# One transformer layer on one core: the gate projection `vg` computed with seven block products instead of eight, with its factors, its row statistics and the spatial weights prepared at other places

## The chip, the cores and the metric

The kernel runs on one core of one Trainium2 chip. TensorE (PE) does the matmuls and the transposes, VectorE (DVE), ScalarE (ACT) and GpSimd (POOL) the element-wise work, and SyncE (SP), POOL and in one place ACT issue the transfers, which 16 DMA engines carry out. The metric is the device time of one execution in microseconds (us), lower is better; several runs are given by their median.

## The reference

One layer of a streaming encoder, `x` of 512 rows (tokens) by 2048, all in fp32:

```python
h = rms_norm(x, g_mix)
proj = h @ w_in                      # 2048 x 9216
q, k, v_sb, u, v_sg, gate_a, gate_b = split(proj, [1024, 1024, 1024, 1024, 1024, 2048, 2048])
y_a = stick_breaking_attention(rms_norm(q), rms_norm(k), v_sb) @ w_oa      # 8 heads
v_sg = gelu(v_sg)
s = gelu(u) * (w_spatial(masked) @ layer_norm(v_sg) + b_spatial)           # 128-token chunks, 8 groups
y_b = s @ w_ob
merged = sigmoid(gate_a) * y_a + sigmoid(gate_b) * y_b
x = x + merged @ w_out
x = x + square(relu(rms_norm(x, g_ff) @ w_ff1)) @ w_ff2
```

The change is about `v_sg` (1024 of the 9216 columns; the kernel calls it `vg`): `rms_norm(x) @ w_in[:, vg]`, its gelu, and the mean and variance of each row that the layer norm needs.

## The kernel before

**Arithmetic.** Every fp32 operand is split in a high and a low part, and a product is the sum of three matmuls: high by high, high by low, low by high (`mm3`, L70 to L74). A weight "piece" is 512 KB, 128 partitions by 1024: it is loaded into a raw tile (pool `raws`, six tiles), ACT casts it to its high part, and DVE takes the difference as its low part (`weight`, L92 to L103; `split_to`, L111 to L117). The parts lie in a pool of three pairs (`w_piece`). Activations lie in `slots`, 64 tiles of 128x512, and in `long`, 12 more. PSUM has five banks for sums (`acc`) and three for side work (`aux`).

**Order of the work.** The program is written in the order of the stages, and each engine runs its instructions strictly in a fixed order, which a scheduler draws up at compile time from a simulated timeline; the transfers of a queue are issued in that order too. Side tasks are put in a queue, `behind`; `step()` (L81) takes one task after each weight piece, or after each of the seven products of a Strassen form. A task's place is thus given by its step.

**Stages.** At the start `x` is loaded in four quarters of 512 columns. `hT_of(k)` (L439) makes the transposed, scaled activations of k-tile k when they are first asked for: four PE transposes into one bank, then two ACT and two DVE instructions of 128x256, whose results are the high and the low part. `by_token` (L122) computes 512 columns of the projection for all four token blocks, eight pieces and 192 matmuls of 128x512 a pass. The first two passes give `v` (8 to 104 us of the profile), and the next two give `vg` (104.4 to 192.75 us), each with 192 matmuls. `evac_v` (L720) then applies the gelu (L722), takes the statistics (`bn_stats`, L723) and puts the result in DRAM (`held_v`, L724).

From 192.76 us on comes a long "run" of gates and attention heads (`strassen_pair`, L277, with `strassen_columns`, L215): for two column tiles and the two halves of the k rows, seven block products in the order y11, m7, m6, y21, m5, m4, y22. The activations of the products are h's own four blocks (y11, y12, y21, y22) and four combinations of them (m7, m6, m4, m5: the "factors", `factor`, L245), kept for eight k pairs. `gate_factors(k)` makes those of one pair: four additions that join high and low part again (`whole`, L514), four sums or differences (L251) and the halves again (ACT and DVE). Before, the eight calls stand at steps 3, 5, ... 17 of the second `v` pass, so most of them fall in the `vg` stage.

Because `long` takes its room from the start, the activations of k-tiles 6, 7 and 8 lie in raw tiles (`hT_both`), and `moved` (L670) copies them to slots by DMA later. The spatial weights are loaded, transposed, masked and split (`load_spatial`, L629; `spatial`, L640) in the second `v` pass. `open_gates` (L715) starts the run's first weight loads in the last step of `vg`.

**The form for rows.** Near the end of the middle part, `w_out` (about 975 to 1125 us) is computed with `strassen_tokens` (L303): four quarters, each with seven products over 1024 weight rows and 1024 columns; a product is 24 matmuls of 128x512. Two of the seven weight operands are sums that DVE makes from raw pieces (L186, L190), and two more are made by transfers that add into a raw tile (POOL queue, L188, L201). Each product's bank is added to one or two of the four results, by ACT where the result is new (L945) and by DVE else (L947).

Of the kernel before, what the change touches and what calls it, by code (L numbers as in the profile page):

```python
# [31 lines left out]
RAWH = 3  # L32
# [3 lines left out]
def tile_hybrid_layer(ctx: ExitStack, tc: tile.TileContext, x, g_mix, w_in, g_q, g_k, ln_g, ln_b,  # L36
# [12 lines left out]
    first = ExitStack()  # L49
    long = first.enter_context(tc.tile_pool(name="long", bufs=LONG))  # L50
# [25 lines left out]
    state = {"load": None, "raw": raws}  # L76
# [362 lines left out]
    def hT_of(k):  # L439

        if k == len(hT):
            t = aux("xT")
            for tb in range(NTB):
                nc.tensor.transpose(out=t[:, tb * P:(tb + 1) * P], in_=xq[tb, k], identity=ident)
# [46 lines left out]
    for k in range(CK):  # L491
# [137 lines left out]
    def load_spatial():  # L629
        for half in range(2):  # L630
            t = slot("ws")
            nc.sync.dma_start(out=t.rearrange("p (g j) -> p g j", g=4),
# [3 lines left out]
            nc.sync.dma_start(out=t, in_=b_sp.rearrange("o g i -> o (g i)")[:, half * W:(half + 1) * W]  # L636
# [3 lines left out]
    def spatial(half):  # L640
        t = aux("wsT")
# [10 lines left out]
        rows = aux("rows")  # L652
        for i in range(2):
# [3 lines left out]
            nc.sync.dma_start(out=held_s[half * 2 + i], in_=f32(pair))  # L657
# [8 lines left out]
        nc.sync.dma_start(out=held_s[4 + half], in_=bs[half])  # L666
# [3 lines left out]
    def moved(k):  # L670
        for half, part in enumerate(hT[k]):
            name = "y" + "12"[k % 2] + "12"[half]
            if LONG // 2 <= k < LONG // 2 + RAWH and name != "y12":
                t = slot("hT", F32R)
                nc.sync.dma_start(out=f32(t), in_=f32(part))
                part = t
            hy[name, k // 2] = part
# [40 lines left out]

    for half in range(2):
        def evac_v(tb, o):  # L720
            t = room.pop() if room else slot("vg")
            state["gelu"] = nc.scalar.activation(out=t, in_=o, func=AF.Gelu, scale=rstd[:, tb:tb + 1])  # L722
            nc.vector.bn_stats(out=stv[:, tb, half * 6:half * 6 + 6], in_=t)  # L723
            nc.gpsimd.dma_start(out=held_v[half, tb], in_=t)  # L724

        if half:
            behind.extend([lambda: None] * (KT // CK - 1 - len(behind)))
            behind.append(open_gates)
        by_token(win, VS + half * W, hT_at, KT, evac_v, "vg", turn=half * LONG // 2)
# [21 lines left out]
    behind.append(moments)  # L751
# [131 lines left out]
    for j in range(D // W):  # L883
        def evac_b(c, o):
# [41 lines left out]
    CHUNK = 4  # L926
    ready = ({"y21": [(0, 0)], "m4": [(0, 1)], "m5": [(1, 1)], "y22": [(1, 0)]}, done[1])

    class Merged:


        def __init__(self, f):
            self.f = f

# [245 lines left out]
```

## Time and profile before

| | us |
|---|---|
| three runs | 2397.48, 2398.22, 2398.96 (median 2398.22) |
| the profiled execution's own time | 2400.23 |
| its span, first to last instruction | 2398.5 |
| opening and `v`, two passes | to 104.4 |
| `vg`, two passes | 104.4 to 192.75 |
| start of the run | 192.76 |

All views are of one profiled execution, with times from the start of its span. A row of a group gives the line, the engine, the operation, what is written and read, the count, then the busy time and the mean duration of one in ns, then the idle time of the engine just before and what ended it. A timeline row gives start, duration, engine, line and operation. A window row gives its length, the busy time of PE, its weight loads, DVE, ACT and POOL with the number of instructions, the granted clock of PE (1.00 is full), the busy share of the DMA engines and GB/s.

### The profile page before, as it was taken

How to read it: one execution, taken by the hardware profiler on the slowest of the kernel's cores; microseconds unless marked ns; L12 is line 12 of the kernel's file. 1: busy time of each engine (PE TensorE's matmuls, PEld its weight loads, DVE VectorE, ACT ScalarE, POOL GpSimd, SP SyncE). 2: the span in 40 equal slices, each digit the busy share in tenths (PEclk: the TensorE clock that was granted, in tenths of full speed). 3: DMA queues.
4: the chain of work that ended last, by engine and by line, in shares of the span. 5: the costliest groups of instructions: out<-in, count | busy, mean ns of one | idle time of the engine just before them, and what ended most of it. 6: DMA issues, size and time to landing. Idle time of an engine off the chain costs nothing.

```text
span 2398.5 us, 34712 instructions
## 1 busy us (share of the span) xinstructions
PE 2382.6 (99%) x12436; PEld 2046.4 (85%) x12436; DVE 1948.1 (81%) x2670; ACT 1340.2 (56%) x2094; POOL 516.6 (22%) x631
## 2 busy tenths in 40 slices
PE   9999999999999999999999999999999999999999
PEld 8888888888888888888988888888888788888887
DVE  5576887778788567778689888898888898998987
ACT  5335676666666323458667777777765343333333
POOL 0101222222222433231000000000024334321210
PEclk9999999999999999999999999999999999999999
DMA  5557888888888945497388888889887999877763
GB/s 185 194 162 161 168 175 188 170 185 171 183 166 191 350 152 180 117 223 198 93 237 229 233 230 226 224 225 230 230 292 264 308 269 318 249 222 213 229 185 96
DMA packets 513037, 498.84 MB, mean 208 GB/s; under 512 B 20896, under 2 KB 398816, under 8 KB 512864
## 3 DMA queue, kind: packets, MB, share of 16 engines
q1 hardware_dynamic: 380880, 332.48, 43.6%
q0 software_dynamic: 131696, 163.61, 33.1%
q8 instruction: 98, 1.61, 0.3%
q10 hardware_dynamic: 288, 0.52, 0.1%
q14 instruction: 75, 0.61, 0.1%
HBM read 405.83 MB, written 89.65 MB: 207 GB/s over the span
## 4 chain that ended last, share of the span: by engine, by line
PE 96%; DMA 1%; DVE 1%; ACT 1%; issue 0%; POOL 0%; SPq 0%; DVEq 0%; ACTq 0%; POOLq 0%
PE q L223 18%; PE fork L223 13%; PE q L73 10%; PE q L74 10%; PE q L72 10%; PE q L226 9%; PE fork L226 7%; PE v L72 1%; PE v L74 1%; PE v L73 1%; PE vg L72 1%; PE vg L74 1%; PE yb L72 1%; PE yb L74 1%; PE yb L73 1%; PE vg L73 1%
## 5 line engine op out<-in xcount | busy, mean ns | idle before, releaser
L113 ACT CAST w_hi<-w_raw 128x1024 fp32r<-128x1024 f32 (+1 forms) x688 | 722.9, 1051 | 774.3 <-PE q L73 373.0
L114 DVE TENSOR_TENSOR w_lo<-w_raw,w_hi 128x1024 fp32r<-128x1024 f32 (+1 forms) x688 | 839.0, 1221 | 213.7 <-ACT w_hi L113 198.4
L73 PE MATMUL q<-w_lo,ys 128*128 128x512 f32 x1120 | 437.4, 391 | 3.7 <-DVE w_lo L114 3.6
L74 PE MATMUL q<-w_hi,ys 128*128 128x512 f32 x1120 | 436.2, 390 | 0.0
L223 PE MATMUL q<-ys,w_hi 128*128 128x512 f32 x1632 | 411.1, 394 | 3.6 <-ACT fork L231 3.6
L72 PE MATMUL q<-w_hi,ys 128*128 128x512 f32 x1120 | 393.1, 390 | 0.2 <-DVE total L1122 0.2
L223 PEld LDWEIGHTS q<-ys,w_hi 128*128 128x128 f32 x1632 | 293.9, 189 | 57.3 <-ACT fork L231 4.4
L73 PEld LDWEIGHTS q<-w_lo,ys 128*128 128x128 f32 x1120 | 210.4, 188 | 49.6 <-DVE w_lo L114 6.3
L72 PEld LDWEIGHTS q<-w_hi,ys 128*128 128x128 f32 x1120 | 210.3, 188 | 43.8 <-issue 0.6
L74 PEld LDWEIGHTS q<-w_hi,ys 128*128 128x128 f32 x1120 | 210.4, 188 | 43.3
L223 PE MATMUL fork<-ys,w_hi 128*128 128x512 f32 x944 | 236.2, 392 | 0.0
L226 PEld LDWEIGHTS q<-ys,w_lo 128*128 128x128 f32 x1632 | 221.3, 191 | 14.1
L188 POOL DMA_DIRECT2D w_raw<-in_w_ff_dram x57 | 79.3, 1392 | 709.7 <-ACT act L1011 160.2
L226 PE MATMUL q<-ys,w_lo 128*128 128x256 f32 x1632 | 228.0, 283 | 0.0
L223 PEld LDWEIGHTS fork<-ys,w_hi 128*128 128x128 f32 x944 | 171.5, 189 | 31.5
L1073 POOL DMA_DIRECT2D ys<-store x224 | 126.7, 578 | 185.9 <-PE q L74 121.8
L186 DVE TENSOR_TENSOR w_raw<-w_raw 128x1024 f32<-128x1024 f32 x98 | 119.7, 1222 | 39.2 <-DMA w_raw<-in_w_in_dram 10.6
L99 ACT CAST w_hi<-w_raw 128x1024 fp32r<-128x1024 f32 x71 | 74.6, 1051 | 120.4 <-issue 36.4
L101 DVE TENSOR_TENSOR w_lo<-w_raw,w_hi 128x1024 fp32r<-128x1024 f32 x71 | 87.7, 1237 | 61.7 <-ACT w_hi L99 59.9
L226 PEld LDWEIGHTS fork<-ys,w_lo 128*128 128x128 f32 x944 | 128.8, 191 | 9.2
L1122 DVE SCALAR_TENSOR_TENSOR total<-q,plus,total 128x512 f32<-128x512 f32 x180 | 132.1, 746 | 4.2 <-PE q L74 4.1
L226 PE MATMUL fork<-ys,w_lo 128*128 128x256 f32 x944 | 131.7, 283 | 0.0
(264 smaller groups left out, 3660.0 us busy)
## 6 DMA issues: line engine op xcount, KB each, us to landing
w_raw<-in_w_ff_dram SPq DMA_DIRECT2D x256, 512.0 KB, 5.8
w_raw<-in_w_in_dram SPq DMA_DIRECT2D x143, 512.0 KB, 5.3
ys<-store POOLq DMA_DIRECT2D x224, 256.0 KB, 6.7
w_raw<-in_w_ff_dram POOLq DMA_DIRECT2D x57, 512.0 KB, 7.0
w_raw<-in_w_in_dram POOLq DMA_DIRECT2D x56, 512.0 KB, 6.5
store<-ys_hi SPq DMA_DIRECT2D x90, 256.0 KB, 5.2
store<-ys_lo SPq DMA_DIRECT2D x90, 256.0 KB, 5.1
w_raw<-in_w_out_dram SPq DMA_DIRECT2D x32, 512.0 KB, 5.2
```

The lines of the kernel that those rows point to most:

```text
L72: nc.tensor.matmul(o, lhsT=lh[0], rhs=rh[0], start=start, stop=False, **kw)
L73: nc.tensor.matmul(o, lhsT=lh[0], rhs=rh[1], start=False, stop=False, **kw)
L74: nc.tensor.matmul(o, lhsT=lh[1], rhs=rh[0], start=False, stop=stop, **kw)
L101: nc.vector.tensor_tensor(out=lo, in0=raw, in1=f32(hi), op=ALU.subtract)
L113: nc.scalar.copy(out=hi, in_=src)
L114: state["lo"] = nc.vector.tensor_tensor(out=lo, in0=src, in1=f32(hi), op=ALU.subtract)
L186: nc.vector.tensor_tensor(out=self.a, in0=self.w11, in1=self.w21, op=ALU.add)
L188: state["sum"] = nc.gpsimd.dma_start(out=self.w21, in_=self.blocks[1, 1], accum_op=ALU.add)
L223: nc.tensor.matmul(o, lhsT=hi[:, k, :], rhs=rhs[name][k], start=name in ("y11", "m7") and k == 0, stop=False, skip_group_check=True)
L226: nc.tensor.matmul(o[:, :HS], lhsT=lo[:, k, :], rhs=rhs[name][k][:, :HS], start=False, stop=k == KH - 1, skip_group_check=True)
L1073: nc.gpsimd.dma_start(out=f32(t), in_=store[f][HELD.index(name), p])
L1122: nc.vector.scalar_tensor_tensor(out=a, in0=o, scalar=part, in1=a, op0=ALU.mult, op1=ALU.add)
```

## The change

1. `vg` is computed by `strassen_tokens`, in two passes over 1024 rows of the weights each, with all 1024 columns: seven products of 24 matmuls a pass. A pass takes the factors of four k pairs. The eight results (`sum`) gather in slots, in pass one and two; the gelu follows when a result is complete, and `bn_stats` is put off to the first eight steps of the run (`moment`).
2. The factors have to be there for it, so `gate_factors` stands at steps 5, 7, 9, 10, 12, 14, 16, 18, counted from the start of `v` (a `v` pass has eight steps). The slots don't suffice for all: of the first four pairs the tiles m6, y21 and m5 (twelve) are written to DRAM (`held_f`) and fetched back into `long` behind `vg`.
3. `long` opens only then; in the opening its room is a pool `more0` of six raw tiles, for the weights of `vg`. All of h lies in slots from the start; `moved` and `hT_both` are gone.
4. `load_spatial` comes after `moments` in the run, `spatial(0)` and `spatial(1)` six and ten steps later, on the banks of `acc`, with their transfers on POOL's queue.
5. The tables of `strassen_tokens` (`takes`, `done`, `ready`) and the class `Chunk` stand further up and serve `vg` and `w_out`.

```diff
+    zero = ExitStack()
+    more = zero.enter_context(tc.tile_pool(name="more0", bufs=6))
...
-            if LONG // 2 <= k < LONG // 2 + RAWH:
-                both = raws.tile([P, 2, W], F32R, name="hT_both", tag="w_raw")
-                parts = [both[:, 0, :], both[:, 1, :]]
-            else:
-                parts = [slot("hT", F32R, long if k < LONG // 2 else slots) for _ in range(2)]
+            parts = [slot("hT", F32R) for _ in range(2)]
...
-        t = aux("wsT")
+        t = acc("wsT")
...
+    PARKED = ("m6", "y21", "m5")
+    held_f = dram.tile([len(PARKED), 4, P, W], F32, name="held_f")
     def gate_factors(k):
+        for i in range(2):
+            for half, part in enumerate(hT[2 * k + i]):
+                hy["y" + "12"[i] + "12"[half], k] = part
         act = [whole(2 * k + i) for i in range(2)]
         for name in ("m7", "m6", "m4", "m5"):
             factor(hy, act, k, name, -1.0 if name in ("m7", "m4") else None)
+        if k < 4:
+            for i, name in enumerate(PARKED):
+                nc.gpsimd.dma_start(out=held_f[i, k], in_=f32(hy[name, k]))
...
-            steps[0].append(load_spatial)
-            steps[2].append(lambda: spatial(0))
-            steps[4].append(lambda: spatial(1))
-            for k in range(KT // 2):
-                steps[3 + 2 * k].append(lambda k=k: gate_factors(k))
...
+    for k, n in enumerate((5, 7, 9, 10, 12, 14, 16, 18)):
+        opening[n].append(lambda k=k: gate_factors(k))
+    opening[29].append(open_gates)
+    at_steps(opening)
...
-        by_token(win, VS + half * W, hT_at, KT, evac_v, "vg", turn=half * LONG // 2)
...
+    def gather(sums, key, o, op, flip=False):
+        if flip:
+            op = ALU.subtract if op == ALU.add else ALU.add
+        if key not in sums:
+            sums[key] = slot("sum")
+            nc.scalar.activation(out=sums[key], in_=o, func=AF.Copy, scale=1.0 if op == ALU.add else -1.0)
+        else:
+            nc.vector.tensor_tensor(out=sums[key], in0=sums[key], in1=o, op=op)
+    vg, moment = {}, []
+    for f in range(2):
+        def evac_v(name, t, o):
+            for half, c, op in takes[name]:
+                gather(vg, (2 * half + t, c), o, op, name in ("m7", "m4"))
+            for half, c in ready[0].get(name, []) if f else []:
+                tb = 2 * half + t
+                g = vg[tb, c]
+                state["gelu"] = nc.scalar.activation(out=g, in_=g, func=AF.Gelu, scale=rstd[:, tb:tb + 1])
+                nc.gpsimd.dma_start(out=held_v[c, tb], in_=g)
+                moment.append(lambda g=g, tb=tb, c=c: nc.vector.bn_stats(out=stv[:, tb, c * 6:c * 6 + 6], in_=g))
+        strassen_tokens(win, f * CHUNK * 2 * P, VS, Chunk(hy, f), evac_v, lambda name: None, twice=True)
+    zero.close()
+    first = ExitStack()
+    long = first.enter_context(tc.tile_pool(name="long", bufs=LONG))
+    for i, name in enumerate(PARKED):
+        for k in range(4):
+            hy[name, k] = fetched(held_f[i, k], "ys", F32R, long)
...
-    behind.append(moments)
+    behind.extend(moment)
+    behind.extend([moments, load_spatial] + [lambda: None] * 5 + [lambda: spatial(0)] + [lambda: None] * 3
+                  + [lambda: spatial(1)])
```

The scheduler's order on three queues shows what moves. On SP's queue in the opening, before, the last three quarters of `x` (`xq`) stand between single pieces of the weights of `v` (`w_raw`); `xk` is the first quarter, `gm` and `gains` are small vectors:

```order
L411 DMA xk<-in_x_dram 128x4x128 x3
L96 DMA w_raw<-in_w_in_dram 128x2x512
L421 DMA xq<-in_x_dram 128x512 x4
L96 DMA w_raw<-in_w_in_dram 128x2x512
L421 DMA xq<-in_x_dram 128x512 x4
L96 DMA w_raw<-in_w_in_dram 128x2x512
L421 DMA xq<-in_x_dram 128x512 x4
L396 DMA gains<-in_g_ff_dram 16x128
```

On the same queue after the change (lines of the changed kernel; L95 loads a piece of `v`, L180 one of `vg`'s first pass into `more0`); three pieces of `v` and the gains stand ahead of these rows:

```order
L95 DMA w_raw<-in_w_in_dram 128x2x512
L420 DMA xq<-in_x_dram 128x512 x4
L95 DMA w_raw<-in_w_in_dram 128x2x512 x3
L180 DMA w_raw<-in_w_in_dram 128x2x512
L95 DMA w_raw<-in_w_in_dram 128x2x512
L180 DMA w_raw<-in_w_in_dram 128x2x512 x3
L95 DMA w_raw<-in_w_in_dram 128x2x512 x2
L420 DMA xq<-in_x_dram 128x512 x8
```

The second quarter of `x` moves behind four pieces, and the third, with the fourth right after it, behind fourteen, of which four are of `vg`.

On ACT in the fifth to seventh pieces of `v`, before, activations (`hT`), squares of `x` (`sq`) and casts of weights (`w_hi`) follow one another:

```order
L436 ACTIVATE sq,ss<-xq 128x512 x4
L116 ACTIVATE hT<-xT,gT 128x256
L99 CAST w_hi<-w_raw 128x1024
L116 ACTIVATE hT<-xT,gT 128x256 x3
L436 ACTIVATE sq,ss<-xq 128x512 x4
```

At the same place after the change, where `whole` and `ys` are the first factors' tiles:

```order
L435 ACTIVATE sq,ss<-xq 128x512 x4
L115 ACTIVATE ys<-whole 128x256
L112 CAST ys<-whole 128x256
L98 CAST w_hi<-w_raw 128x1024
L115 ACTIVATE ys<-whole 128x256
L112 CAST ys<-whole 128x256
L115 ACTIVATE hT<-xT,gT 128x256 x4
```

The activations of k-tiles 12 and 13, the last row, now stand behind four instructions of the factors and behind a cast of a weight piece.

On POOL's queue from the end of `vg` into the run, before, the eight results go to DRAM and the run's adding transfers (L188, L201) follow:

```order
L724 DMA held_v<-vg 128x512 x4
L188 DMA w_raw<-in_w_in_dram 128x8x128
L724 DMA held_v<-vg 128x512 x4
L201 DMA w_raw<-in_w_in_dram 128x8x128
L737 TENSOR_TENSOR rv<-ve,mhalf 128x4
```

The same place after the change, with the adding transfers of `vg`'s second pass (128x2x512) and the twelve fetches (L509):

```order
L743 DMA held_v<-sum 128x512 x2
L200 DMA w_raw<-in_w_in_dram 128x2x512 x2
L187 DMA w_raw<-in_w_in_dram 128x8x128
L743 DMA held_v<-sum 128x512 x2
L509 DMA ys<-held_f 128x512 x12
L743 DMA held_v<-sum 128x512 x3
L200 DMA w_raw<-in_w_in_dram 128x8x128
L743 DMA held_v<-sum 128x512
L760 TENSOR_TENSOR rv<-ve,mhalf 128x4
```

The fetches stand among the results of the second pass, ahead of the last four, and ahead of the run's second adding transfer.

More of the change, by code (lines that the diff above doesn't have):

```diff
@@ L74, in mm3 @@
         nc.tensor.matmul(o, lhsT=lh[1], rhs=rh[0], start=False, stop=stop, **kw)
-    state = {"load": None, "raw": raws}
+    state = {"load": None, "raw": raws, "more": more}
     behind = collections.deque()
@@ L635, in load_spatial @@
             t = slot("bs")
-            nc.sync.dma_start(out=t, in_=b_sp.rearrange("o g i -> o (g i)")[:, half * W:(half + 1) * W]
+            nc.gpsimd.dma_start(out=t, in_=b_sp.rearrange("o g i -> o (g i)")[:, half * W:(half + 1) * W]
                               .to_broadcast([P, W]))
@@ L656, in spatial @@
             split_to(p3[:, :, 0, :], p3[:, :, 1, :], m3[:, 2 * i:2 * i + 2, :])
-            nc.sync.dma_start(out=held_s[half * 2 + i], in_=f32(pair))
+            nc.gpsimd.dma_start(out=held_s[half * 2 + i], in_=f32(pair))
             r2 = rows[:, i * 2 * P:(i + 1) * 2 * P].rearrange("p (g i) -> p g i", g=2)
@@ L665, in spatial @@
                                            in1=bs[half][:, c], op0=ALU.mult, op1=ALU.add)
-        nc.sync.dma_start(out=held_s[4 + half], in_=bs[half])
+        nc.gpsimd.dma_start(out=held_s[4 + half], in_=bs[half])
     hy = {}
[L670 to L677, printed above, removed]
+    PARKED = ("m6", "y21", "m5")
+    held_f = dram.tile([len(PARKED), 4, P, W], F32, name="held_f")
     def gate_factors(k):
+        for i in range(2):
+            for half, part in enumerate(hT[2 * k + i]):
+                hy["y" + "12"[i] + "12"[half], k] = part
         act = [whole(2 * k + i) for i in range(2)]
@@ L726, in tile_hybrid_layer, with evac_h @@
-        if half:
-            behind.extend([lambda: None] * (KT // CK - 1 - len(behind)))
-            behind.append(open_gates)
-        by_token(win, VS + half * W, hT_at, KT, evac_v, "vg", turn=half * LONG // 2)
+        def evac_h(tb, o):
+            for i, part in enumerate(split(o, "v", rstd[:, tb:tb + 1])):
+                nc.gpsimd.dma_start(out=held_a[i, half, tb], in_=f32(part))
+        by_token(win, VC + half * W, hT_at, KT, evac_h, "v")
+    CHUNK = 4
+    takes = {"y11": [(0, 0, ALU.add)], "y21": [(0, 0, ALU.add)], "m7": [(1, 1, ALU.add)],
+             "m6": [(0, 1, ALU.subtract)], "y22": [(1, 0, ALU.add)], "m4": [(0, 1, ALU.add)],
+             "m5": [(1, 1, ALU.subtract), (1, 0, ALU.add)]}
@@ new lines, in tile_hybrid_layer, with __init__, __getitem__ @@
+    done = ({"y21": [(0, 0)], "m4": [(0, 1)], "m5": [(1, 1), (1, 0)]},
+            {"m5": [(1, 1)], "y22": [(1, 0)], "m4": [(0, 1)], "y21": [(0, 0)]})
+    ready = ({"y21": [(0, 0)], "m4": [(0, 1)], "m5": [(1, 1)], "y22": [(1, 0)]}, done[1])
+    class Chunk:
+        def __init__(self, ys, f):
+            self.ys, self.f = ys, f
+        def __getitem__(self, name):
+            return [sides(self.ys[name, self.f * CHUNK + k]) for k in range(CHUNK)]
+    def gather(sums, key, o, op, flip=False):
[6 more added lines that the diff above has]
+            nc.vector.tensor_tensor(out=sums[key], in0=sums[key], in1=o, op=op)
@@ L924, in input_factors @@
             factor(hs, act, k, name, -1.0 if name in ("m7", "m4") else None, pool)
[L926 to L933, printed above, removed]
-        def __getitem__(self, name):
-            return [sides(ms[name, self.f * CHUNK + k]) for k in range(CHUNK)]
     for f in range(2):
@@ L941, in evac_x @@
                 for half, c, op in takes[name]:
[L942 to L947 removed]
+                    gather(x2, (2 * half + t, 2 * g + c), o, op)
                 for half, c in ready[g].get(name, []) if f else []:
@@ L965, in between_x @@
                                                 accum_op=ALU.add)
-            strassen_tokens(w_out[0], f * CHUNK * 2 * P, g * 2 * W, Merged(f), evac_x, between_x, last=f == 1 and g == 1,
+            strassen_tokens(w_out[0], f * CHUNK * 2 * P, g * 2 * W, Chunk(ms, f), evac_x, between_x, last=f == 1 and g == 1,
                             twice=True)
```

45 lines of the change are left out of this document (8 added, 37 removed).

## The prediction

> **What bounds the kernel now.** I read the page's busy times, its row of granted clocks and its chain, then PE's waits over the whole span, then windows of the stages that the change touches, then timelines of PE around `vg` and in the opening.
>
> ```profile
> span 2398.5 us, 34712 instructions
> PE 2382.6 (99%) x12436; PEld 2046.4 (85%) x12436; DVE 1948.1 (81%) x2670; ACT 1340.2 (56%) x2094; POOL 516.6 (22%) x631
> PEclk9999999999999999999999999999999999999999
> PE 96%; DMA 1%; DVE 1%; ACT 1%; issue 0%; POOL 0%; SPq 0%; DVEq 0%; ACTq 0%; POOLq 0%
> PE q L73 <- DVE w_lo L114: 3.6, 5, 1.6
> PE q L223 <- ACT fork L231: 3.6, 4, 1.3
> PE ya L72 <- DVE merged_a L873: 1.7, 2, 1.3
> ```
>
> PE is busy 99% of the span at full clock, and it is 96% of the chain. Its three largest waits sum to 9 us, and none of them lies in `vg`. So a matmul less is time less, as long as what feeds PE keeps up. The windows of `vg`, of a stretch of the run and of `w_out`, which has the form that `vg` now gets:
>
> ```profile
> 104.00:193.00 89.00, 89.00 (x398) 73.82 (x397) 62.68 (x123) 36.05 (x59) 9.59 (x16) 1.00 0.53 163
> 230.00:260.00 30.00, 30.00 (x179) 26.66 (x178) 21.61 (x32) 18.78 (x33) 9.31 (x6) 1.00 0.91 176
> 980.00:1080.00 100.00, 100.00 (x443) 82.88 (x442) 78.24 (x100) 54.91 (x78) 33.63 (x35) 1.00 0.79 193
> ```
>
> PE is full in all three. In `w_out` the form runs beside a DVE that is busy 78 of 100 us, and PE waits for nothing.
>
> **What is saved.** `vg` has 384 matmuls of 128x512 (two passes of 192). The new form has 7 products x 2 weight sums x 2 token halves x 2 k-tiles x 3 = 168 a pass, 336 in all, 48 fewer; the order lists just these. PE's timeline gives the price of one by the distance of starts:
>
> ```profile
> 185.73 0.39 PE L74 MATMUL vg<-w_hi,hT 128*128 128x512 f32 x1
> 192.53 0.39 PE L74 MATMUL vg<-w_hi,hT 128*128 128x512 f32 x1
> ```
>
> There are thirty matmuls from the first start to the second, 6.80 us, so one takes 0.2267 us (0.39 is its length in the pipeline). 48 x 0.2267 = 10.9 us saved. A pass takes 168 x 0.2267 = 38.1 us.
>
> **DVE in the new `vg`.** The durations are in these groups (`vg`'s stage, the gathering of `w_out`, the spatial weights), and a piece of DVE's timeline in `w_out`:
>
> ```profile
> L101 DVE TENSOR_TENSOR w_lo<-w_raw,w_hi 128x1024 fp32r<-128x1024 f32 x14 | 17.1, 1224 | 13.1 <-ACT w_hi L99 13.0
> L251 DVE TENSOR_TENSOR whole<-whole 128x256 f32<-128x256 f32 x28 | 11.8, 423 | 0.7
> L518 DVE TENSOR_TENSOR whole<-hT 128x256 f32<-128x256 f32 x22 | 7.9, 418 | 0.0
> L114 DVE TENSOR_TENSOR ys<-whole,ys 128x256 fp32r<-128x256 f32 x14 | 5.9, 422 | 2.4 <-ACT ys L113 2.4
> L947 DVE TENSOR_TENSOR x<-x,q 128x512 f32<-128x512 f32 x32 | 21.1, 681 | 1.8 <-PE q L74 1.4 <-issue 0.2
> L117 DVE SCALAR_TENSOR_TENSOR v_lo<-v,rstd,v_hi 128x512 fp32r<-128x512 f32 x4 | 2.7, 743 | 0.0
> ...
> 1044.71 1.22 DVE L186 TENSOR_TENSOR w_raw<-w_raw 128x1024 f32<-128x1024 f32 x1
> 1045.84 1.22 DVE L114 TENSOR_TENSOR w_lo<-w_raw,w_hi 128x1024 fp32r<-128x1024 f32 x1
> 1046.98 0.68 DVE L947 TENSOR_TENSOR x<-x,q 128x512 f32<-128x512 f32 x1
> 1047.58 1.22 DVE L186 TENSOR_TENSOR w_raw<-w_raw 128x1024 f32<-128x1024 f32 x1
> ```
>
> Pass one has 14 low parts and 4 weight sums at 1.22 (22.0), 8 gathering adds at 0.68 (5.4; the eight first touches are ACT's), the factors of two k pairs, twelve instructions at 0.42 each (10.1), and four low parts of `v` at 0.74 (3.0): 40.5 us in a pass of 38.1. That would be too much, but the timeline's starts are 1.13 and 0.60 apart, 0.09 less than the durations, and 54 instructions x 0.09 = 4.9, which leaves 35.6. So DVE is the next engine in line, some 94% full, with three pairs of parts as its only buffer. I take 0 lost, bounds 0 to 3 (40.5 - 38.1 = 2.4, plus a wait of the size of the largest above). Below zero it can't go, since PE has no wait in `vg` to lose. Pass two has 22.0 and 16 adds (10.9), 32.9 of 38.1: nothing lost.
>
> **From `vg` to the run.** The twelve tiles that were put in DRAM are fetched through POOL's queue and land in `long`. The nearest rows are the fetches of `ys` late in the kernel, then the run's start:
>
> ```profile
> L1073 POOL DMA_DIRECT2D ys<-store x224 | 126.7, 578 | 185.9 <-PE q L74 121.8
> ys<-store POOLq DMA_DIRECT2D x224, 256.0 KB, 6.7
> ...
> 192.76 1.98 PE L223 MATMUL q<-hT,w_hi 128*128 128x512 f32 x8
> 195.52 2.00 PE L223 MATMUL q<-ys,w_hi 128*128 128x512 f32 x8
> 198.32 2.00 PE L223 MATMUL q<-ys,w_hi 128*128 128x512 f32 x8
> ```
>
> Issuing takes 12 x 0.58 = 7.0 us and a landing 6.7 us. In the order they stand behind the fourth of eight results. The product y22 comes last in `vg`, with 24 x 0.2267 = 5.4 us, and the results of m4 and m5 are ready ahead of it, so the fetches begin 6 to 8 us before the run. The first tile (m6) is used two products after the run's start, 198.32 - 192.76 = 5.6 us, and its four have landed by about -7 + 2.3 + 6.7 = 2 us. I take 0.3 for this seam. If they could only begin with the run, m6 would come at 2.3 + 6.7 = 9.0 and wait 3.4; that is the upper bound. What is queued behind them on POOL: four results and the run's second adding transfer, whose sum is for the seventh product (y22), 6 x 2.8 = 17 us into the run.
>
> In the run the deferred statistics and the spatial weights come to DVE and PE. By
>
> ```profile
> L646 DVE COPY wsm<-wsT 64x512 f32<-64x512 f32 x1 | 0.7, 683 | 0.9 <-PE wsT L643 0.9
> L664 DVE SCALAR_TENSOR_TENSOR bs<-rows,gT,bs 128x128 f32<-128x128 f32 x4 | 1.1, 340 | 0.0
> ```
>
> a half has two copies (1.4), two low parts (0.8) and four sums (1.4), 3.6 us of DVE, of which the run's stretch above leaves free 30 - 21.61 = 8.4 in 30 us. Their PE work only moves. The statistics move from `vg` as well. I take 0.2, bounds -1 (less in a fuller stage) to 1.5 (one wait of the run's kind). Seam and run: 0.5.
>
> **The opening.** Here I expect the price. The factors themselves need x early, yet the order puts the third and fourth quarter of x behind fourteen weight pieces.
>
> ```profile
> 0.00:12.00 12.00, 9.92 (x50) 8.60 (x51) 3.96 (x7) 6.13 (x12) 1.72 (x14) 1.00 0.90 272
> 8.00:18.00 10.00, 10.00 (x51) 8.31 (x51) 7.82 (x14) 7.14 (x14) 0.00 (x0) 1.00 1.05 386
> 20.00:30.00 10.00, 10.00 (x51) 8.23 (x49) 4.75 (x9) 3.20 (x6) 0.00 (x0) 1.00 0.53 161
> 7.74 3.23 SPq L421 DMA_DIRECT2D xq<-in_x_dram  x4
> xq<-in_x_dram SPq DMA_DIRECT2D x12, 256.0 KB, 6.6
> 32.81 1.25 PE L444 MATMUL xT<-ident,xq 128*128 128x128 f32 x10
> 33.82 0.49 PE L72 MATMUL v<-w_hi,hT_both 128*128 128x512 f32 x1
> ```
>
> Up to 12 us the DMA engines move 272 GB/s, 3.26 MB, and then, with a busy share of 1, 386 GB/s. Before, 4.7 MB are asked for up to the third quarter (eight x loads of 0.26 beside the first quarter's 1.05 and three pieces of 0.52): 12 + 1.44 / 0.386 = 15.7 us. Its last load was issued at 7.74 + 3.23 = 10.97 and took 6.6, so it landed at 17.6, a lag of 1.9 us on this sum, and 15 us before PE transposes it, at 32.81.
>
> After: 1.05 + 1.05 + 1.05 for three quarters, 14 x 0.524 pieces on SP, 0.52 on ACT: 11.0 MB, which takes until 12 + 7.74 / 0.386 = 32.1, and with the lag until 34.0. In the same stretch POOL's queue carries four parked tiles of h (1.05 MB, 2.7 us) and one adding transfer (0.52 MB, 1.4 us); if all of it goes ahead of x, 38.1. PE's transposes of k-tile 8 stand at the same matmul as before, due at 32.81, so the wait is 1.2 to 5.3 us. I take the middle, 3.3, since the quoted stretch has one queue's loads alone and says nothing of how two share. The Trainium skill, page "DMA: Bandwidth & Descriptors", section "Issuing engines are not separate DMA queues", says that transfers of all issuing engines run on the same 16 DMA engines and interleave; by it the 1.57 MB count nearly whole, the wait would be 5.3, and the sum 2 us higher.
>
> DVE and ACT stand in x's way as well:
>
> ```profile
> L116 ACT ACTIVATE hT<-xT,gT 128x256 fp32r<-128x256 f32 x25 | 11.0, 468 | 4.0 <-DVE hT L117 4.0
> L117 DVE SCALAR_TENSOR_TENSOR hT<-xT,gT,hT 128x256 fp32r<-128x256 f32 x25 | 11.5, 478 | 5.7 <-ACT hT L116 5.7
> L99 ACT CAST w_hi<-w_raw 128x1024 fp32r<-128x1024 f32 x10 | 10.5, 1046 | 2.9 <-DMA w_raw<-in_w_in_dram 2.2 <-ACT hT L116 0.6
> L431 DVE TENSOR_REDUCE ss<-sq 128x4 f32<-128x512 f32 x4 | 2.5, 678 | 0.0
> ```
>
> Ahead of k-tile 8's part on DVE stand two weight sums of `vg`, two low parts, one part of h and four reductions: 4 x 1.22 + 0.48 + 4 x 0.68 = 8.1 us behind the landing of `vg`'s third load, 8.4 MB into the queue, 12 + 5.1 / 0.386 + 1.9 = 27.2: 35.3, about when x is there too, so this is the same wait and not another. On ACT k-tile 12's parts stand behind four factor instructions (0.41 each) and a cast of a piece of the second `v` pass, whose buffer comes free only with step five's last matmuls. If the cast starts with step five's end, PE waits 1.05 + 2 x 0.41 + 0.47 + 0.48 = 2.8; if PE's matmuls of the step's end cover it, 0. I take 1.4. Opening: 4.7, bounds 1.2 to 8.1.
>
> **The sum.** -10.9 + 4.7 + 0.5 = -5.7 us: 2394.5 for an execution like the profiled one (2400.23), which lies 2.0 above the median of the runs, so 2398.22 - 5.7 = 2392.5.
>
> **Rivals.** *B, the opening costs under 2.5 us.* For: before, x was there 15 us ahead, and the loads ahead of x may be held up less than summed. Against: the bytes. It gives 2398.2 - 10.9 + 0.5 to 2.5, 2387.8 to 2390.3. *C, a seam in `vg` or behind it.* DVE falls behind in pass one (2.4 to 3), or the fetches are late (3.4), on top of the opening's 4.7: 2394.5 to 2398. For: 94% load, in-order queues; against: `w_out` runs the form without a wait. *D, slower: x's third quarter comes after 41.8.* The change breaks even where the opening's wait for k-tile 8 is 10.9 - 1.4 - 0.5 = 9.0, 32.8 + 9.0 = 41.8. Up to 20 us 6.35 MB are moved; the other 4.65 MB then need 234 GB/s or less from 20 us to 39.9. At 20 to 30 us before, only 161 GB/s were moved, because loads waited for raw tiles; the new order too has more pieces ahead of x than the twelve raw tiles hold, so its last piece waits for a cast, and x behind it. At 200 GB/s x lands at 20 + 23.3 + 1.9 = 45.2, a wait of 12.4, and the time is 2401.6. Against: only the last pieces need a tile that was used before, and those of the first steps are free by then. *E, PE slows down after the gap.* Before, the clock is full in every slice, and the longest wait is 1.6 us, so no row shows what a wait of 3 to 5 us does; if PE ran at half pace for as long as the wait of 3.3 took, that would add 3.3, 2395.8. The Trainium skill, page "TensorE: Matmul & The Clock Gate", section "Why this matters for your kernels", asks for no idle gap of over about 3 us between matmuls and says that one idle window takes the clock to half; this gap is at its edge, and no trace here shows it. *F, that it isn't done:* the order has 336 matmuls, so this is out.
>
> **How the numbers follow.** The forecast (opening 2.5 to 6.5 in all, 2390.3 to 2394.3) has 0.52, B 0.21, C 0.14, D 0.07, E 0.06. 0.2% is 4.8 us, about what a measurement can tell: faster means under 2393.4, slower over 2403.0. Faster: B and four fifths of the forecast, 0.62. Slower: the upper part of D, 0.04. The rest, 0.34, is same. The range 2388 to 2397.5 leaves out B's lower end, C's upper and D, about 0.18.
>
> **What would show it.** Right: some 12390 matmuls, a stage of `vg` of about 76 us without a wait of PE, a wait of `xT` for the DMA `xq` of 1 to 5 us near 33 to 38 us, one of `v` for ACT's `hT` some 10 us later, nothing at the run's start over 1 us, clock full. Wrong: no wait for `xq` (B), waits of PE for `w_lo` in `vg`, or for `ys` in the run's first 12 us (C), a wait for `xq` of 9 us or more (D), a slice with a lower clock (E).

## The result, and the profile after

The changed kernel takes 2411.22 us (median of 4 runs, 2408.05 to 2413.97) against 2398.59 us before (4 runs, 2397.48 to 2399.52): 12.6 us slower, a ratio of 1.0052 with a 95% interval of 1.0035 to 1.0070. The forecast was 2392.5, with a range up to 2397.5. Its runs also lie further apart than those of before, 5.9 us against 2.0. The profiled execution took 2413.97 us, its span is 2412.3: it is the slowest of the four. Its mean granted clock is 0.996, that of the others 0.998, 0.998 and 0.999, so what the profile shows of a slower clock is more than the median execution has.

The page's span, busy times and chain of the changed kernel:

```profile
span 2412.3 us, 34793 instructions
PE 2382.2 (99%) x12388; PEld 2040.9 (85%) x12388; DVE 1982.3 (82%) x2714; ACT 1357.2 (56%) x2114; POOL 544.6 (23%) x673
PE 93%; DMA 3%; DVE 2%; ACT 1%; issue 1%; POOL 0%; SPq 0%; ACTq 0%; DVEq 0%; POOLq 0%
```

There are 48 matmuls less, as said, and yet PE is busy for as long as before (2382.2 against 2382.6). PE's idle time, span less busy time, has grown from 15.9 to 30.1 us. So two things have to be found: 14.2 us of waits, and some 10.5 us by which PE's busy time for the remaining matmuls grew. PE's waits in the first 300 us show the first (the row left out, 1.2 us ahead of the first instruction, stands in both kernels):

```profile
PE xT L443 <- DMA xq<-in_x_dram: 3.8, 3, 1.8
PE fork L222 <- ACT fork L230: 3.0, 1, 3.0
PE rows L658 <- ACT wsp L112: 2.6, 1, 2.6
PE v L71 <- DVE v_lo L116: 1.5, 1, 1.5
PE xT L443 <- DMA xk<-in_x_dram: 1.4, 2, 0.8
...
PE v L73 <- DVE hT L116: 1.1, 1, 1.1
PE v L71 <- ACT w_hi L98: 1.0, 2, 0.7
PE v L71 <- ACT hT L115: 0.9, 2, 0.5
PE v L72 <- DVE w_lo L100: 0.8, 1, 0.8
```

Before, this stretch had 2.9 us of waits in all. Now 10.5 us lie in the opening (the waits of `xT` and `v`), 3.0 at the run's product y22 (`fork`), 2.6 at the spatial weights (`rows`). None lies in `vg`. The windows show the second; the column before the last two is the granted clock:

```profile
35.11:38.52 3.41, 0.73 (x2) 0.30 (x2) 3.41 (x6) 0.95 (x1) 0.95 (x1) 1.00 1.02 283
38.52:45.35 6.83, 5.83 (x19) 4.30 (x20) 3.86 (x7) 2.17 (x5) 0.00 (x0) 0.50 0.93 285
118.00:194.00 76.00, 76.00 (x337) 62.76 (x336) 65.82 (x89) 41.74 (x52) 17.64 (x24) 1.00 0.69 172
212.60:216.01 3.41, 1.06 (x5) 0.88 (x6) 2.24 (x5) 2.65 (x4) 0.09 (x1) 1.00 0.12 37
216.01:219.43 3.42, 3.42 (x14) 2.99 (x13) 3.42 (x6) 1.71 (x3) 1.54 (x1) 0.50 0.31 35
260.39:263.80 3.41, 1.20 (x10) 0.96 (x8) 3.27 (x7) 0.07 (x1) 0.00 (x0) 1.00 0.90 221
263.80:270.63 6.83, 6.44 (x22) 5.67 (x23) 5.80 (x11) 2.62 (x5) 3.66 (x4) 0.50 0.56 184
```

Behind each of the three places with the most idle time the clock is at half, for 6.83, 3.41 and 6.83 us. PE is busy for 15.7 us of these 17.1, so about 7.8 us are lost there. Of the 10.5 us this leaves 2.7. Most of it lies at the stops themselves: in a full row the next matmul starts 0.2267 us after the last one, but ahead of a stop the last one counts as busy for its whole 0.39. The trace has 32 stops of PE, that of before 18, and 14 x 0.16 = 2.3 us.

The stages, by the last matmul of `v` and the first of the run; first before, whose run begins at 192.76, then after:

```profile
103.78 0.39 PE L74 MATMUL v<-w_hi,hT 128*128 128x512 f32 x1
```

```profile
117.90 0.39 PE L73 MATMUL v<-w_hi,hT 128*128 128x512 f32 x1
194.63 1.98 PE L222 MATMUL q<-hT,w_hi 128*128 128x512 f32 x8
```

`v` ends 14.1 us later. `vg` takes 76.7 us where it took 89.0, which is 12.3 less: the 10.9 of 48 matmuls, and PE's work for the spatial weights, part of which lay there before. So at the run's start the change is 1.9 us behind. The first score matmul `z` of the attention comes at 285.8, before at 270.3, 15.5 us later: 13.6 are lost in the run's first 91 us. Behind `z` 1.8 us come back, most of it in shorter waits.

### The profile page after: what moved, and what is told of

Its sections match the earlier page's. It is cut to its first block, busy times and chain, and to the rows that moved or that the text cites. A ratio compares the mean times of both kernels' runs of the same rounds, so it can differ in the third digit from the quotient of the medians.

```text
span 2412.3 us, 34793 instructions
## 1 busy us (share of the span) xinstructions
PE 2382.2 (99%) x12388; PEld 2040.9 (85%) x12388; DVE 1982.3 (82%) x2714; ACT 1357.2 (56%) x2114; POOL 544.6 (23%) x673
## 4 chain that ended last, share of the span: by engine, by line
PE 93%; DMA 3%; DVE 2%; ACT 1%; issue 1%; POOL 0%; SPq 0%; ACTq 0%; DVEq 0%; POOLq 0%
PE q L222 17%; PE fork L222 13%; PE q L72 11%; PE q L73 11%; PE q L71 11%; PE q L225 9%; PE fork L225 6%; DMA w_raw<-in_w_in_dram 2%; PE yb L72 1%; PE yb L71 1%; PE yb L73 1%; PE ya L71 1%; PE ya L73 1%; PE ya L72 1%; PE v L71 1%; PE v L72 1%
## 5 line engine op out<-in xcount | busy, mean ns | idle before, releaser
L112 ACT CAST w_hi<-w_raw 128x1024 fp32r<-128x1024 f32 (+1 forms) x716 | 752.3, 1051 | 795.2 <-PE q L72 396.4
L113 DVE TENSOR_TENSOR w_lo<-w_raw,w_hi 128x1024 fp32r<-128x1024 f32 (+1 forms) x716 | 872.2, 1220 | 208.0 <-ACT w_hi L112 189.3
L72 PE MATMUL q<-w_lo,ys 128*128 128x512 f32 x1184 | 461.7, 390 | 3.7 <-DVE w_lo L113 3.6
L73 PE MATMUL q<-w_hi,ys 128*128 128x512 f32 x1184 | 460.6, 389 | 0.0
L71 PE MATMUL q<-w_hi,ys 128*128 128x512 f32 x1184 | 415.6, 390 | 0.2 <-DVE total L1124 0.2
L222 PE MATMUL fork<-ys,w_hi 128*128 128x512 f32 x1056 | 267.1, 393 | 0.0
L71 PEld LDWEIGHTS q<-w_hi,ys 128*128 128x128 f32 x1184 | 222.2, 188 | 46.8 <-issue 0.6
L73 PEld LDWEIGHTS q<-w_hi,ys 128*128 128x128 f32 x1184 | 222.3, 188 | 45.9
L225 PEld LDWEIGHTS q<-ys,w_lo 128*128 128x128 f32 x1632 | 221.4, 190 | 14.2
L222 PEld LDWEIGHTS fork<-ys,w_hi 128*128 128x128 f32 x1056 | 190.6, 189 | 34.1
L185 DVE TENSOR_TENSOR w_raw<-w_raw 128x1024 f32<-128x1024 f32 x102 | 124.6, 1223 | 63.8 <-DMA w_raw<-in_w_in_dram 31.3
L225 PEld LDWEIGHTS fork<-ys,w_lo 128*128 128x128 f32 x1056 | 146.0, 190 | 11.5
L225 PE MATMUL fork<-ys,w_lo 128*128 128x256 f32 x1056 | 149.6, 282 | 0.0
L189 DVE TENSOR_TENSOR w_raw<-w_raw 128x1024 f32<-128x1024 f32 x102 | 124.8, 1223 | 6.4 <-DMA w_raw<-in_w_ff_dram 5.2
```

The costliest lines, as they stand in the source:

```text
L71: nc.tensor.matmul(o, lhsT=lh[0], rhs=rh[0], start=start, stop=False, **kw)
L72: nc.tensor.matmul(o, lhsT=lh[0], rhs=rh[1], start=False, stop=False, **kw)
L73: nc.tensor.matmul(o, lhsT=lh[1], rhs=rh[0], start=False, stop=stop, **kw)
L112: nc.scalar.copy(out=hi, in_=src)
L113: state["lo"] = nc.vector.tensor_tensor(out=lo, in0=src, in1=f32(hi), op=ALU.subtract)
L185: nc.vector.tensor_tensor(out=self.a, in0=self.w11, in1=self.w21, op=ALU.add)
```

## The experiments

Four theories: **Q**, SP's order brings x late. **F**, the factors' and squares' work on ACT and DVE stands in front of the casts and the last parts that PE waits for. **T**, the fetches crowd the transfers that the run's first pairs need. **S**, the spatial weights at that place. Against all of them stands a clock that falls behind a gap, whatever made the gap. In the table, "to before" is the difference of medians, each to the runs of before in the same comparison; the other columns are of the profiled execution: the end of `v`'s last matmul, the time from there to the first `z`, and the time at half clock (without the last 4 us of the kernel).

| kernel | median, us | to before | v ends | to z | half clock |
|---|---|---|---|---|---|
| before | 2398.59 | | 104.2 | 166.1 | 0 |
| changed | 2411.22 | +12.6 | 118.3 | 167.5 | 17.1 |
| x_order | 2405.13 | +6.4 | 112.3 | 166.9 | 10.2 |
| y22_dve | 2404.97 | +6.2 | 116.1 | 164.1 | 13.7 |
| spatial_late | 2408.39 | +9.6 | 118.8 | 159.8 | 13.7 |
| three | 2396.13 | -2.7 | 110.1 | 155.4 | 0 |
| both | 2399.23 | +0.4 | 104.8 | 165.2 | 3.4 |
| fetch4 | 2407.05 | +8.3 | 118.2 | 160.2 | 13.7 |
| warm | 2412.80 | +14.0 | 117.0 | 165.4 | 6.8 |
| nowarm | 2411.37 | +12.6 | 118.2 | 163.7 | 13.7 |
| tuned | 2391.73 | -6.6 | 104.6 | 158.1 | 3.4 |
| pool | 2410.17 | +11.8 | 104.5 | 176.1 | 20.5 |
| tuned_pool | 2407.47 | +9.1 | 106.6 | 172.1 | 13.7 |
| tuned8 | 2388.57 | -9.9 | 105.1 | 154.3 | 0 |

**x_order.** x's quarters at their old places: every later weight load on SP is put behind the x load written ahead of it.

```diff
+        with tc.issue_after(state["x"].ins) if state.get("x") else nullcontext():
             state["load"] = nc.sync.dma_start(...)
...
-            nc.sync.dma_start(out=t, in_=x[tb * P:(tb + 1) * P, q * 512:(q + 1) * 512])
+            state["x"] = nc.sync.dma_start(out=t, in_=x[tb * P:(tb + 1) * P, q * 512:(q + 1) * 512])
```

> The changed kernel with x's second to fourth quarter loaded at their old places on SP's queue; nothing else. Theory Q (the queue's order made x late, PE idled at k-tiles 4, 8 and 10 and ran at half clock from 38.5 to 45.3 us): the waits for xq (3.8), for hT (1.5) and the 3 us of the half clock go, 2401 to 2404, and no half clock before 200 us. Rival F (the factors' work on ACT and DVE in the v stage is what delays PE): most of the 14 us of the opening stays, 2408 or more.

It is 6.3 us nearer to before than the changed kernel, less than Q expected and more than rival F, and `v` ends 6.0 sooner. All waits for `xq` are gone, but others stay or come out from behind them, as PE's waits up to 130 us show:

```profile
PE v L71 <- ACT w_hi L99: 2.5, 2, 1.8
PE xT L445 <- DMA xk<-in_x_dram: 1.5, 2, 1.0
PE v L71 <- DVE v_lo L117: 1.5, 1, 1.5
...
PE v L72 <- DVE w_lo L101: 0.8, 1, 0.8
PE v L71 <- ACT hT L116: 0.5, 1, 0.5
```

The wait of 1.8 us is new: from 29.2 us on PE waits for a cast that stands on ACT behind four squares of x's first quarter, and 3.4 us at half clock follow, against what Q expected. So Q holds for its own waits, and 8.1 of the 14.1 us are left, for F and for the first quarter's wait of 1.5.

**y22_dve.** The run's first sum for y22 by DVE, without the adding transfer.

```diff
-        w = column_sums(win, US, twice=True)
+        w = column_sums(win, US)
```

> The changed kernel, with the run's first sum for y22 made by DVE (1.2 us) and not by an adding transfer. Theory T (the adding transfer took 11.5 us beside the twelve fetches, ACT stood at its cast, and the copy for PE behind it): the wait of 3.0 near 212 us goes and the half clock of 3.4 us behind it too, 2406 to 2407.5. Rival L (everything at the run's start is late, also ACT and DVE): PE waits there for another low part, and 1.5 us or less are gained, 2409.5 to 2411.

6.4 us nearer to before, more than expected. The wait of 3.0 and its half clock are gone; a wait of 1.7 for a low part has come in its place, below what costs clock. From `v`'s end to `z` it is 3.5 us, and of the rest 2.2 are an opening that was shorter in this execution, which the edit doesn't touch. T's mechanism is right; its size lies between 3.5 and 6.4.

**fetch4.** Only the four tiles of m6 are fetched. For the first four k pairs the products y21 and m5 read y22's tiles instead, so this kernel leaves out the eight other fetches and computes other numbers; its matmuls are as many.

```diff
-            hy[name, k] = fetched(held_f[i, k], "ys", F32R, long)
+            hy[name, k] = fetched(held_f[i, k], "ys", F32R, long) if name == "m6" else hy["y22", k]
```

> The changed kernel, with only the four m6 tiles fetched; the products y21 and m5 take the tiles of y22 for the first four k pairs, so its gates, q and k are other numbers. Theory T (the adding transfer for y22 lands late because eight more fetches of 256 KB share the DMA engines): it lands in 7 to 9 us and not 11.5, PE waits less than 1 us there, 4 to 5 us less than the changed kernel, 2406 to 2407.5. Rival L (ACT and DVE bring the transfer's issue too late): the wait of 3 us stays.

4.4 us nearer, as T expected, and no wait of `fork` is left at y22. POOL's timelines show the adding transfer, first in the changed kernel, then in fetch4:

```profile
201.76 1.60 POOL L200 DMA_DIRECT2D w_raw<-in_w_in_dram  x1 [0.24 <-issue]
```

```profile
197.89 1.60 POOL L200 DMA_DIRECT2D w_raw<-in_w_in_dram  x1 [0.44 <-DVE w_lo L113]
```

`v` ends alike in both, so it is issued 3.9 us sooner, and it lands in 7.9 us where the changed kernel's took 11.5; before, with no fetches, the same transfer took 7.6. Rival L falls, since the wait doesn't stay. But not all of it is the sharing of the DMA engines: eight fetches fewer bring the issue forward as well as the landing.

**spatial_late.** The spatial weights late in the run.

```diff
-    behind.extend([moments, load_spatial] + [lambda: None] * 5 + [lambda: spatial(0)] + [lambda: None] * 3
-                  + [lambda: spatial(1)])
+    behind.extend([moments] + [lambda: None] * 166 + [load_spatial] + [lambda: None] * 8 + [lambda: spatial(0)]
+                  + [lambda: None] * 5 + [lambda: spatial(1)])
```

> The changed kernel with the spatial weights prepared some 480 us later in the run. Theory S (the preparation fills DVE at 260 us, PE waits 2.6 for its rows and is at half clock for 6.8 us): 5 to 6 us less, 2405 to 2406.5, with PE full and at full clock from 250 to 280 us. Rival D (DVE is late there anyway, from adding transfers of 9 us): another wait takes its place, less than 2 us gained.

3.0 us nearer, half of what S expected, and more than rival D's less than 2. At the place itself S is right, PE is full and at full clock there:

```profile
255.00:285.00 30.00, 30.00 (x175) 26.46 (x175) 23.45 (x35) 19.61 (x36) 7.01 (x7) 1.00 0.87 179
```

To `z` 7.7 us are gained, of which 1.8 are PE work that only moves. But in this execution the opening's wait of 1.5 us for `v_lo`, with one of 0.8 ahead of it, cost a stretch at half clock that the changed kernel's profile doesn't have, and a wait ahead of `ya` grew from 0.4 to 1.4. What goes wrong at that place in the changed kernel, DVE's timeline shows:

```profile
257.98 1.12 DVE L662 SCALAR_TENSOR_TENSOR bs<-rows,gT,bs 128x128 f32<-128x128 f32 x4
259.01 1.21 DVE L189 TENSOR_TENSOR w_raw<-w_raw 128x1024 f32<-128x1024 f32 x1
...
262.21 0.68 DVE L644 COPY wsm<-wsT 64x512 f32<-64x512 f32 x1
```

The copy `wsm`, on which PE's `rows` wait, comes 3 us behind the first half's sums, since a weight sum, a low part and an attention part stand between them. DVE has no gap there, though in the 30 us shown of before it had 8. The changed kernel has one too, but ahead of it: from 251.3 to 254.3 us DVE stands still for a weight load, and its work is that much later behind it.

**three.** These edits together: x_order, y22_dve and spatial_late.

> The three edits together. If the costs are apart and add up (9 in the opening, 4.7 at y22, 6 at the spatial weights): 2391 to 2393, faster than before by 6. If they overlap or a next wait follows each: 2396 to 2402. No half clock before the last 4 us in the first case.

The three single gains, 6.3, 6.4 and 3.0, sum to 15.7; together they bring 15.3 (ratio to before 0.9991, 0.9982 to 1.0001). So the costs lie apart and add up. The time itself lies in the range that was given for overlapping costs, 2396 to 2402, and not in the 2391 to 2393 of this case, because two of the single gains were smaller than reckoned. From `v`'s end to `z` little is left to gain: 155.4 us are 10.7 less than before. What is left is in the opening, `v` ends 6.0 late.

**both.** The factors after the first `v` pass, and squares of x's first quarter sooner, on top of three.

```diff
-lambda: load_x(1), lambda: None, lambda: load_x(2), lambda: (load_x(3), squares(0), load_gains()),
+lambda: load_x(1), lambda: squares(0), lambda: load_x(2), lambda: (load_x(3), load_gains()),
...
-    for k, n in enumerate((5, 7, 9, 10, 12, 14, 16, 18)):
+    for k, n in enumerate((9, 10, 11, 12, 13, 14, 16, 18)):
```

> The three edits, and the factors made at steps 9, 10, 11, 12, 13, 14, 16, 18 of the opening, not from step 5 on, and the squares of x's first quarter two steps sooner. Theory F (what is left of the opening, v ending at 110.1 us and not at 104.2, is ACT's and DVE's factor work and squares ahead of casts and of v's last parts): PE's five waits of 0.5 to 1.8 us before 70 us go, v ends near 105, and the time is 2390 to 2391.5. Rival V (the factors, now denser, fill DVE in the second v pass and vg): waits for w_lo there, 2394 to 2397.

F is right on the opening: `v` ends at 104.8, nearly as before. And rival V is right on the rest, and low: 9.8 us come back behind it, and the time, 2399.23, lies above both ranges. PE's waits from 100 to 220 us:

```profile
PE q L227 <- DVE w_lo L114: 2.1, 1, 2.1
PE q L71 <- ACT sum L732: 2.1, 1, 2.1
PE q L71 <- ACT w_hi L113: 1.9, 2, 1.0
PE q L72 <- DVE w_lo L114: 1.2, 2, 0.7
```

The first pass of `vg` was reckoned 94% full on DVE; with the second `v` pass filled by six sets, nothing is left to catch up in. That is argued: the waits show that low parts and casts come late, and no run separates DVE from ACT here.

**tuned.** One set in the first `v` pass, the second set a step later, so that it stands behind `v`'s results; else as both.

```diff
-    for k, n in enumerate((9, 10, 11, 12, 13, 14, 16, 18)):
+    for k, n in enumerate((5, 8, 9, 10, 12, 14, 16, 18)):
```

> The three edits, x's first squares sooner, and the factors at steps 5, 8, 9, 10, 12, 14, 16, 18: one set in the first v pass, the second not in its last step, ahead of v's results, but behind them. Theory B (DVE's and ACT's work of the opening and of vg is one sum that just fits; what is late at a pass's end costs, what is spread does not): v ends at 105 to 107 us, vg has no wait over 1 us and no half clock, 2391 to 2393. Rival V (any set moved out of the first v pass comes back as waits in vg): v ends sooner, vg later, 2394 to 2397.

2391.73 us, as theory B expected (8 runs, ratio 0.9973, 0.9963 to 0.9984): `v` ends at 104.6, and `vg` has no wait at all. The early squares were tried only together with such steps. Behind `vg` the longest wait is 1.9 us at the second pair, whose weights land late (DVE waits 5.6 us for them), with half clock behind it.

**pool and tuned_pool.** The four additions of a set that join high and low parts on POOL; pool with the steps of both, tuned_pool with those of tuned.

```diff
-            nc.vector.tensor_tensor(out=t[:, half * HS:(half + 1) * HS], in0=hi, in1=lo, op=ALU.add)
+            nc.gpsimd.tensor_tensor(out=t[:, half * HS:(half + 1) * HS], in0=hi, in1=lo, op=ALU.add)
```

> The kernel with all factors from step 9 on, and the four additions of each set that join high and low parts made on POOL and not on DVE (32 x 0.42 = 13 us less on DVE up to vg's first pass, some 0.7 us each on POOL). Theory B (DVE's fullness makes the waits in vg): the waits of 5.2 us in vg and the half clock there go, v ends at 105 us, 2389 to 2392. Rival Q (POOL's queue, with the parked tiles and the adding transfers behind the additions, delays the weight sums): waits in vg stay, 2396 or more.

> Both: the steps 5, 8, 9, ... and the additions on POOL. Theory B: like the faster of the two or 1 us below, 2389 to 2391.5; rival Q: 2394 or more.

Theory B falls: pool is 11.4 us slower than both, tuned_pool 15.7 slower than tuned. The times lie in rival Q's ranges, but its reason isn't shown. Taking 13 us of work off DVE didn't unload it, for DVE stands still while POOL adds (pool, the timelines of DVE and of POOL):

```profile
105.00 3.02 DVE L117 SCALAR_TENSOR_TENSOR ys<-whole,ys 128x256 fp32r<-128x256 f32 x1 [0.48 <-ACT ys L116]
107.95 0.41 DVE L114 TENSOR_TENSOR ys<-whole,ys 128x256 fp32r<-128x256 f32 x1
```

```profile
104.92 2.82 POOL L518 TENSOR_TENSOR whole<-hT 128x256 f32<-128x256 f32 x4
```

An instruction that takes 0.42 us takes 3.02, until POOL's four additions are over. In all of pool the 16 DVE instructions that run beside these additions take 18.4 us longer than the medians of their kinds, more than the 13 that were taken off. Whether the order of POOL's queue, where the additions stand behind the parked tiles, costs anything besides, no run separates.

**warm and nowarm.** Meant to keep PE at work in the gap before the spatial rows: the rows two steps behind their split, in warm with twelve spare matmuls ahead.

```diff
+    def spatial_rows(half, fill=0):
+        rows = acc("rows")
+        with tc.issue_after(state["pe"].ins):
+            for n in range(fill):
+                nc.tensor.matmul(rows, lhsT=ones_r, rhs=hy["y11", 0], start=True, stop=True)
```

> The changed kernel with the spatial rows in a task two steps behind their split, and twelve matmuls on data that nobody uses directly ahead of the first rows, on PE in the time in which it would wait. Theory C (an idle stretch of PE of 2 to 3 us halves the clock for 3.4 or 6.8 us): the wait is 0 to 0.5, no half clock from 255 to 285 us, and it is 2.5 to 4 us faster than the same kernel without the twelve. Rival N (the half clock comes from something else at that place, the load of all engines or the transfers): the half clock stays, and the two are alike.

> The same without the twelve matmuls, the one to compare with. Both theories: like the changed kernel, PE waits 2 to 3 us for the rows near 262 us and has the half clock behind it, 2409 to 2412.

Inconclusive. In warm the clock is full from 255 to 285 us, as C expected, but in nowarm too: with the rows in a task of their own, PE no longer waits for them there either, against both theories, and a wait of 2.8 us for a cast at 234.7 takes its place. The two medians are 1.4 us apart the other way, within the runs' spread. So the half clock wasn't taken away by an experiment that leaves the gap's place; what speaks for its cause is below.

**tuned8.** tuned, with y21 kept in its slots: eight tiles go to DRAM and come back.

```diff
-    PARKED = ("m6", "y21", "m5")
+    PARKED = ("m6", "m5")
```

> The kernel with the factors at 5, 8, 9, ..., with only eight tiles put in DRAM and fetched (m6 and m5 of the first four pairs; y21 stays in its slots). Theory T (the fetches crowd the DMA engines at the run's start, so that the second pair's weights land late, DVE stands 5.6 us and PE 1.9): that wait falls under 1 us, no half clock follows, 2388.5 to 2390.5. Rival L (the weights are late for another reason): the wait stays, 2391 to 2393.

2388.57 us (5 runs, 2387.84 to 2390.51), 9.9 less than before, a ratio of 0.9961 (0.9948 to 0.9975). T is right. The page and PE's waits up to 300 us:

```profile
span 2386.9 us, 34742 instructions
PE 2372.4 (99%) x12388; PEld 2037.4 (85%) x12388; DVE 1984.3 (83%) x2715; ACT 1355.8 (57%) x2114; POOL 540.0 (23%) x664
...
PE q L224 <- ACT fork L232: 1.0, 1, 1.0
PE v L72 <- DVE w_lo L101: 0.8, 1, 0.8
PE v L71 <- ACT hT L116: 0.5, 1, 0.5
```

PE's busy time is now 10.2 us below that of before, its idle time, 14.5, a little below too. This is close to the 10.9 that 48 matmuls at 0.2267 us are worth where nothing waits for the rest of the change.

## Why the prediction was wrong

- **Saved, 10.9: right.** `vg`'s stage is 12.3 us shorter in the changed kernel, and tuned8 is 9.9 us faster than before.
- **DVE in `vg`, 0: right** for the changed kernel: 65.8 of 76 us busy and no wait of PE. Its two halves have 33.9 and 31.9 us where 35.6 and 32.9 were worked out. The worry about the first pass was not idle, as both shows.
- **Seam, 0.3: wrong.** The step asked when m6's tiles come, and they came in time. It put the adding transfer behind them at nothing because its sum is needed only 17 us into the run. It was issued 7.1 us into the run and took 11.5 (before, 7.6), so it came 18.7 us after the run's start. The cast on ACT waited for it, and the copy for PE behind the cast: 3.0 us, and 1.7 at half clock.
- **Spatial weights, 0.2 (-1 to 1.5): wrong.** DVE's free share over 30 us (8.4) was taken for free time where it is needed. There was none in these 6 us: 2.6 us of wait, 3.2 at half clock.
- **Opening, 4.7 (1.2 to 8.1): mis-sized, 14.1.** The transfer sum was too short. It had x's third quarter land, with the last of its four loads, between 34.0 and 38.1 us. PE's transposes show that the first load was there at 38.60 and the last at 41.54:

```profile
38.60 2.15 PE L443 MATMUL xT<-ident,xq 128*128 128x128 f32 x9 [1.78 <-DMA xq<-in_x_dram]
41.54 0.90 PE L443 MATMUL xT<-ident,xq 128*128 128x128 f32 x3 [0.79 <-DMA xq<-in_x_dram]
```

  The upper end counts POOL's bytes in full, as the Trainium skill has it, page "DMA: Bandwidth & Descriptors", section "Issuing engines are not separate DMA queues". The trace agrees with it: from 12 to 38.1 us all queues together move 355 GB/s, no more than the 386 that SP's loads had alone before. At 355 the 12.6 MB of the upper end take until 38.2, and the last load landed 3.3 us behind that, where 1.9 was taken. So the step that failed here is the rate and the lag. The wait at this place, 2.6 us, lies within the 1.2 to 5.3 all the same, and that is luck: x came 3.4 us behind the upper end, and PE was 4 us late itself. Rival D's mark, x behind 41.8, was missed by 0.3 us. PE was late by waits that were costed at nothing: 1.4 on the first quarter, 1.2 on the second, 1.5 on activations. Of the factors' work only one cast was costed. Their place at the end of the first `v` pass, ahead of `v`'s last parts, was not: three against tuned gives 5.5 us for it and the squares together. In sum the opening has 9.8 us more of waits than before and loses 2.9 at half clock; the rest is mostly at the stops.
- **Rival E, 0.06 at 3.3 us: far too low.** It came true at three places in the profile, 7.8 us; without it this execution would still be 5.9 us slower than the profiled one of before (13.7 - 7.8), so the sign of the forecast would have been wrong even so. The range took in neither this nor a sum of several late things. Each rival was one wait, in C on top of the opening's, and the forecast needed all of them to be small at once.

What stays open: an experiment that removes the half clock alone, and how the 5.5 us divide between the factors' place and the squares.

## What to carry to other kernels

A step that saves work on the busiest engine has to be paid for in what feeds it: add up DVE, ACT and the DMA bytes of the stages ahead of it, not only of the stage that is changed, and look at what stands right in front of the instruction that PE waits for. A load of some 90% is fine while the work comes in evenly, and a mean over 30 us says nothing of a 3 us gap. Behind such a gap count the slower clock as well.

## What the runs showed of the hardware

**The clock looks at windows, not at gaps.** This is worked out from the traces. Every stretch at half clock in the 14 profiles, but the last one of each kernel, which its end cuts off, is 3.41 us long or a whole multiple of it. I cut each profile into windows of 3.413 us, aligned to a change of its clock, and summed PE's idle time in each. Without those of each kernel's end, all 18 windows with 1.82 us or more are followed by half clock; of eight at 1.80 to 1.81, six; and of the windows at full clock with 0.9 to 1.67 us, over 70, one (1.11 us, in fetch4). A gap of nowarm shows it:

```profile
232.73:236.14 3.41, 1.94 (x13) 1.57 (x11) 0.75 (x1) 1.00 (x2) 1.58 (x1) 1.00 1.05 320
236.14:239.56 3.42, 2.11 (x9) 1.77 (x10) 2.21 (x3) 3.27 (x7) 0.00 (x0) 1.00 1.27 187
239.56:242.97 3.41, 3.41 (x23) 3.09 (x23) 3.38 (x5) 1.05 (x1) 0.00 (x0) 1.00 0.23 48
```

It is 2.79 us long, and a window's edge divides it in two (1.47 and 1.31 idle), so the clock stays. Another one there, of 1.82 us at 298.4, lies in one window, and the next runs at half. The clearest case is the same row of waits in two kernels: 0.68, 0.76 and 1.52 us at the end of the first `v` pass. In the changed kernel (first two rows) an edge falls such that 1.44 and 1.52 us lie in two windows, and the clock stays; in spatial_late (last two) 1.80 us of idle time fall in one window, and the next is at half:

```profile
72.66:76.07 3.41, 1.97 (x7) 1.05 (x6) 2.09 (x4) 1.57 (x4) 0.60 (x1) 1.00 0.12 16
76.07:79.49 3.42, 1.90 (x9) 1.55 (x9) 3.30 (x6) 2.48 (x5) 2.45 (x5) 1.00 0.95 343
72.92:76.33 3.41, 1.61 (x6) 0.86 (x5) 2.71 (x6) 1.66 (x4) 0.75 (x2) 1.00 0.40 97
76.33:79.74 3.41, 2.93 (x7) 2.36 (x8) 3.41 (x9) 1.38 (x3) 3.41 (x7) 0.50 0.96 368
```

So the same wait costs half of 3.4 us in one execution and nothing in the next, by where the window's edge falls, and this fits the wider spread of the changed kernel's runs. The Trainium skill, page "TensorE: Matmul & The Clock Gate", section "What's actually happening", has the window (3413 ns, free-running), and the trace agrees with it. The advice in the page's section "Why this matters for your kernels", no gap over some 3 us, is too wide here: 1.82 us in one window was enough each time.

**POOL's additions stop DVE.** While POOL runs a set of these additions (four, 128x256, two operands in SBUF), a DVE instruction can stand until the whole set is over: 3.02 us instead of 0.42, and the low part of a weight piece up to 4.29 instead of 1.22. Six of the 16 in pool are held for more than 1.5 us in this way. At other places the two take turns, and POOL is the slower one: its set at 129.05 us takes 4.72 instead of 2.82. tuned_pool shows the same, with 16 DVE instructions and 17.0 us more.
